# Gated DeltaNet decay matrices spread by TensorE, systems stored pair by pair, two solve steps per grain

## Chip, cores and metric

The kernel runs on one core of one Trainium2 chip. The metric is the device time of one execution in microseconds (us). Everything is float32; matmuls that are written with the type float32r take rounded operands, and a value is then carried as a rounded part and a remainder ("hi" and "lo").

## Reference, cut to what matters

A decoder trunk of two layers over 512 positions and 1024 features: windowed attention, feed-forward, gated DeltaNet, feed-forward. The change lies in the DeltaNet, which works on 16 heads (8 pairs that share a key head) and chunks of 64 positions:

```python
gc = jnp.cumsum(g, axis=-1)
decay = jnp.exp(jnp.where(incl, gc[..., :, None] - gc[..., None, :], -jnp.inf))
kk = jnp.einsum("bhncd,bhnsd->bhncs", k, k)
m = jnp.where(strict, beta[..., :, None] * kk * decay, 0.0)
a = m + jnp.eye(C, dtype=f32)
sol = lax.linalg.triangular_solve(a, rhs, left_side=True, lower=True, unit_diagonal=True)
qk = jnp.where(incl, jnp.einsum("bhncd,bhnsd->bhncs", q, k) * decay, 0.0)
# then a scan over the chunks: v_new = u - w S; o = q_dec S + qk v_new; S = S * g_last + k_dec^T v_new
```

## The kernel before, in words

Activations stand transposed, 128 features on the partitions and 512 positions along a row. Positions are cut into NB = 4 blocks of 128 (two chunks each).

**Dense work.** A weight tile of 128x1024 is loaded (L133), rounded by ScalarE (`whi`, L134), and VectorE makes the remainder (`wlo`, L135); `mm3` (L143) then issues three matmuls of 512 columns for each of 8 slices (L145, L146, L147), 24 to a tile. The three weight buffers turn over. The DeltaNet projects 48 such tiles in `gdn` (L653): 8 for k, then 24 for z and q in the order `zzqzzqzzqzzqzzzzzzzzqqqq` (L724), then 16 for v (L735). The output projection is 16 tiles in two halves (L741 to L768).

**Order.** Smaller jobs are Python generators in a queue. `dense` (L149) calls `pump` (L93) after every second slice, so a tile has four *grains*; a generator that yields n comes back n grains later. `until` (L102) pumps without dense work until something is ready. So the program order of the small jobs against the dense tiles is counted in grains; the tile framework turns program order, with its own estimate of what is ready, into one instruction order for each engine, which the chip then keeps. All loads and stores are issued by one queue, SP (SyncE).

**The jobs around the change.** `gates` (L576) makes the cumulated log decays `gc` (positions on partitions, blocks and heads along a row), turns them (L640) and stores the turned rows in DRAM as `rowd` (L644). `decays` (L772) then goes through the 8 pairs: four products of keys (`kk`, L807); for each of the two heads a DMA copies the head's 512 decays from `rowd` onto all 128 partitions of a buffer `D` (L799, one pair ahead; two buffers); VectorE subtracts `gc` and adds the mask `low` block by block (L810, 8 a pair); ScalarE takes the exponential of all 1024 columns at once (L812); `D` is stored (L813), multiplied into `kk` by VectorE (`kd`, L818) and stored (L820). A pair takes 6 grains (two times `yield 3`). `solve` (L825) loads the diagonal 32x32 blocks of all 16 heads and 8 chunks from the stored `kd` into `X` (L839, four DMAs, 128-byte pieces), scales them (L841), and makes 30 elimination steps of two VectorE instructions (L846, L848), one step a grain; then it stores the inverse and its transpose in a key-position layout (`T`, L854; `N`, L862). `recur` (L865) goes through the pairs: `prologue` (L888) loads `kk`, `D`, `kt`, `qd` (L900 to L903), waits for the solve and 16 grains more, loads `N` and `T` (L911, L914) and finishes the inverse with small matmuls (L923 to L961); it also waits for `rq`, which comes 10 grains after the last q tile, and for the pair's v; `chain` (L973) is the scan, `epilogue` (L1016) the gated norm. `post_qk` (L668) and `post_v` (L688) do convolution (L560 to L563), transposition (`turn`, L565) and norms for each projected tile.

Of the kernel before, what the change touches and what calls it, by code (L numbers as in the profile page):

```python
# [10 lines left out]
F32 = mybir.dt.float32  # L11
# [6 lines left out]
P = 128  # L18
T = 512
NB = 4  # L20
# [6 lines left out]
def layout(x, positions, mixer_norm, ffn_norm, attn_w_in, attn_q_gain, attn_k_gain, attn_sinks,  # L27
           attn_w_out, gdn_w_in, gdn_conv, gdn_a_log, gdn_dt_bias, gdn_norm, gdn_w_out,
           ffn_w_up, ffn_conv, ffn_conv_b, ffn_w_down):

    c = np.ascontiguousarray
    a = {}
    a["xT"] = c(x[0].T.reshape(KT, P, T))
    a["up"] = c(ffn_w_up.reshape(2, KT, P, 2, 24, P).transpose(0, 4, 3, 2, 1, 5)).reshape(2, 24, 2, P, 1024)
    a["down"] = c(ffn_w_down.reshape(2, 3, 8, P, 8, P).transpose(0, 1, 4, 3, 2, 5)).reshape(2, 3, 8, P, 1024)
    cols = []
    cols.append(mixer_norm.reshape(2, KT, P).transpose(2, 0, 1).reshape(P, 16))
    cols.append(ffn_norm.reshape(2, KT, P).transpose(2, 0, 1).reshape(P, 16))
    cols.append(ffn_conv.reshape(2, 3, 24, P).transpose(3, 0, 2, 1).reshape(P, 144))
    cols.append(gdn_conv[0].reshape(4, 32, P).transpose(2, 1, 0).reshape(P, 128))  # L40
    cols.append(gdn_norm[0].reshape(P, 1))
    cols.append(ffn_conv_b.reshape(2, 24, P).transpose(2, 0, 1).reshape(P, 48))
    w = attn_w_in[0]
    w = np.concatenate([w[:, 1024:1280], w[:, :512], w[:, 1280:], w[:, 512:1024]], axis=1)
    a["win"] = c(w.reshape(2, 4, P, 6, 256).transpose(3, 0, 2, 1, 4)).reshape(6, 2, P, 1024)
    wo = attn_w_out[0].reshape(2, 2, 4, 64, D).transpose(0, 2, 1, 3, 4).reshape(KT, P, KT, P)
    a["wout"] = c(wo.reshape(2, 4, P, KT, P).transpose(0, 3, 2, 1, 4)).reshape(2, KT, P, 512)
    a["rows"] = c(np.concatenate([attn_q_gain[0], attn_k_gain[0], attn_sinks[0]]))
    a["pos"] = c(positions[0].reshape(NB, P).T)
    a["freq"] = (500000.0 ** (-np.arange(0, 16, 2, dtype=np.float64) / 16)).astype(np.float32)  # L50
    i, j = np.arange(P)[:, None], np.arange(2 * P)[None]
    a["band"] = np.where((i + P - j >= 0) & (i + P - j < P), 0.0, -1e30).astype(np.float32)
    a["cols"] = c(np.concatenate(cols, axis=1))
    w = gdn_w_in[0].reshape(KT, P, -1).transpose(1, 0, 2)
    a["gin"] = c(w[:, :, :6144].reshape(P, KT, 48, P).transpose(2, 0, 1, 3)).reshape(48, P, 1024)
    a["gba"] = c(w[:, :, 6144:]).reshape(P, KT * 32)
    a["gout"] = c(gdn_w_out[0].reshape(2, 8, P, KT, P).transpose(0, 3, 2, 1, 4)).reshape(2, KT, P, 1024)
    a["grow"] = c(np.concatenate([gdn_a_log[0], gdn_dt_bias[0]]))
    a["tri"] = c(np.triu(np.ones((P, P), np.float32)))
    a["low"] = np.where(np.arange(P)[None] < np.arange(P)[:, None], -1e30, 0.0).astype(np.float32)  # L60
    a["ident"] = np.eye(P, dtype=np.float32)
    return a


# [3 lines left out]
class Builder:  # L68
# [507 lines left out]
    def gates(self, u, ready):  # L576
# [2 lines left out]
        V = nc.vector  # L579
        flat = lambda t: t.rearrange("p n h -> p (n h)")  # L580
        tri = gx.tile([P, P], F32, name="tri")
        self.low = gx.tile([P, P], F32, name="low")
        full = gx.tile([P, P], F32, name="full")
        grow = gx.tile([P, 32], F32, name="grow")
        self.aux.dma_start(tri, self.ins["tri"])
        self.aux.dma_start(self.low, self.ins["low"])
        self.aux.dma_start(grow, self.ins["grow"].partition_broadcast(P))
        V.memset(full, 1.0)
        hi, lo = self.weight(self.ins["gba"], 256)
        ps = self.psum()  # L590
        for k in range(KT):
# [48 lines left out]
        nc.tensor.transpose(pt[:, 0:P], both.rearrange("p i n h -> p (i n h)"), self.ident)  # L640
        bt = gx.tile([P, P], F32, name="bt")
        V.tensor_copy(bt, pt[:, 0:P])
        self.rowd = self.dram.tile([2, NB, 16, P], F32, name="rowd")
        self.aux.dma_start(self.rowd.rearrange("i n h c -> (i n h) c"), bt)  # L644
        ready.add("gates")
# [7 lines left out]
    def gdn(self, h, hd, stack, after):  # L653
# [5 lines left out]
        u, self.u = self.u, []  # L659
        d = self.d = {nm: dram(nm + "d", [8, P, 2, NB, P]) for nm in ("v", "z", "D")}  # L660
        d["kt"] = dram("ktd", [8, P, T])
        d["kk"], d["T"], d["N"] = dram("kkd", [P, 16, NB, P]), dram("Td", [P, 16, NB, 32]), dram("Nd", [P, 16, NB, 32])
        d["bk"] = dram("bkd", [2, 16, NB, 64])
        kT, qT = self.kT, self.qT = [], []
        ss = {"k": self.hub("ssk", 8), "q": self.hub("ssq", 8)}
# [43 lines left out]
        sp = st.enter_context(self.tc.tile_pool(name="sp", bufs=1, reuse_waits="tile"))  # L709
        sy = ExitStack()  # L710
        xp = sy.enter_context(self.tc.tile_pool(name="xp", bufs=1, side="right", reuse_waits="tile"))
        self.spawn(self.decays(sp, ready))
        self.spawn(self.solve(xp, ready))
        outs = {}

        def enter():
# [52 lines left out]
        st.close()  # L769
        return hp  # L770

    def decays(self, sp, ready):  # L772

        nc = self.nc
        V = nc.vector
# [17 lines left out]
        for m in range(2):  # L793
            self.aux.dma_start(d["bk"][m].rearrange("h n c -> n h c"), bt[:, m * 64:m * 64 + 64])

        def rows(hk):
            D = sp.tile([P, 2, NB, P], F32, tag="D", name="D", bufs=2)
            for j in range(2):
                self.aux.dma_start(D[:, j], self.rowd[0, :, 2 * hk + j].partition_broadcast(P))  # L799
            return D  # L800

        D = rows(0)
        for hk in range(8):
            kk = self.psum()
            for n in range(NB):
                s = slice(n * P, (n + 1) * P)
                nc.tensor.matmul(kk[:, s], self.kT[hk][:, s], self.kT[hk][:, s], start=True, stop=True)  # L807
            for j in range(2):
                for n in range(NB):
                    V.scalar_tensor_tensor(D[:, j, n], D[:, j, n], gc[:, n, 2 * hk + j:2 * hk + j + 1], self.low,  # L810
                                           op0=ALU.subtract, op1=ALU.add)
            nc.scalar.activation(D, D, AF.Exp)  # L812
            self.aux.dma_start(d["D"][hk], D)  # L813
            nxt = rows(hk + 1) if hk < 7 else None
            yield 3
            kd = sp.tile([P, 2, NB, P], F32, tag="kd", name="kd", bufs=2)
            for n in range(NB):
                V.scalar_tensor_tensor(kd[:, :, n], kk[:, n * P:(n + 1) * P].unsqueeze(1).broadcast_to([P, 2, P]), rk[:, n, hk:hk + 1],  # L818
                                       D[:, :, n], op0=ALU.mult, op1=ALU.mult)
            self.aux.dma_start(d["kk"][:, 2 * hk:2 * hk + 2], kd)  # L820
            D = nxt
            yield 3
        ready.add("systems")

    def solve(self, sp, ready):  # L825

        nc = self.nc
        V = nc.vector
        d = self.d
        while "systems" not in ready:  # L830
            yield 1
        X = sp.tile([P, 2, 32, 32], F32, name="X")
        bk = sp.tile([P, 2, 32], F32, name="bk")
        for m in range(2):
            ms = slice(m * 64, m * 64 + 64)
            self.aux.dma_start(bk[ms], d["bk"][m].rearrange("h n (i c) -> (h n) i c", i=2))
            for i in range(2):
                q = slice(m * 64 + i * 32, m * 64 + i * 32 + 32)
                self.aux.dma_start(X[ms, i], d["kk"][q, :, :, q].rearrange("s h n c -> (h n) s c"))  # L839
        for i in range(2):  # L840
            V.tensor_tensor(X[:, i], X[:, i], bk[:, i:i + 1].broadcast_to([P, 32, 32]), op=ALU.mult)  # L841
        yield 1
        for j in range(1, 31):
            w = 31 - j
            tm = sp.tile([P, 480], F32, name="tm")[:, :2 * j * w].rearrange("p (i s c) -> p i s c", i=2, c=w)
            V.tensor_tensor(tm, X[:, :, :j, j:j + 1].broadcast_to([P, 2, j, w]),  # L846
                            X[:, :, j:j + 1, j + 1:].broadcast_to([P, 2, j, w]), op=ALU.mult)
            V.tensor_tensor(X[:, :, :j, j + 1:], X[:, :, :j, j + 1:], tm, op=ALU.add)  # L848
            yield 1
        nc.gpsimd.memset(X.rearrange("p i s c -> p i (s c)")[:, :, ::33], 1.0)  # L850
        for m in range(2):
            for i in range(2):
                q = slice(m * 64 + i * 32, m * 64 + i * 32 + 32)
                self.aux.dma_start(d["T"][q].rearrange("s h n c -> (h n) s c"), X[m * 64:m * 64 + 64, i])  # L854
        for i in range(2):
            for b in range(2):
                nat = self.t2().rearrange("p (c s) -> p c s", s=32)
                cs = slice(b * 16, b * 16 + 16)
                nc.scalar.copy(nat, X[:, i, :, cs].rearrange("p s c -> p c s"))
                for m in range(2 - i):  # L860
                    q = slice(m * 64 + i * 32 + b * 16, m * 64 + i * 32 + b * 16 + 16)
                    self.aux.dma_start(d["N"][q].rearrange("s h n c -> (h n) s c"), nat[m * 64:m * 64 + 64])  # L862
        ready.add("solved")

    def recur(self, rx, ready, outs):  # L865
# [22 lines left out]
    def prologue(self, rx, hk, ready):  # L888
# [19 lines left out]
        for a in range(3):  # L908
            q = slice(a * 32, a * 32 + 32)
            c = slice(32, 64) if a == 1 else slice(0, 32)  # L910
            self.aux.dma_start(NT[q, :, :, c].rearrange("p j n c -> p (j n) c"), d["N"][q, hs].rearrange("p j n c -> p (j n) c"))  # L911
        for a in range(4):
            q = slice(a * 32, a * 32 + 32)
            self.aux.dma_start(TT[q, :, :, q].rearrange("p j n c -> p (j n) c"), d["T"][q, hs].rearrange("p j n c -> p (j n) c"))  # L914
        yield 3
        jn = [(j, n) for j in range(2) for n in range(NB)]

# [187 lines left out]
```

## Time and profile before

| | |
|---|---|
| time, median of 3 runs | 1582.84 us (1579.8 to 1583.84) |
| the profiled execution's own time | 1579.06 us |
| its span, first to last instruction | 1577.3 us |
| mean granted TensorE clock | 0.971 |
| DeltaNet, by its weight casts | about 577 to 1160 us of the span |

The page of the profile gives busy times of the engines, PE = TensorE's matmuls, PEld its weight loads, DVE = VectorE, ACT = ScalarE, POOL = GpSimd, SP = SyncE, and what ended each engine's idle time. "DVE D L810 <- DMA D<-rowd" reads: VectorE's instruction of line 810 that writes D waited for the DMA that writes D from rowd. Matmuls are pipelined, so the duration of one is longer than the distance from one to the next. A granted clock of 1.00 is 2.4 GHz; its lower level is 1.2 GHz, and a mean between shows how much of a stretch was at each.

### The profile page before, as it was taken

The numbers are of one execution on the slowest core, as the hardware profiler recorded it, in microseconds if no ns is written. First come the engines' busy times: TensorE is split into PE (matmuls) and PEld (weight loads), VectorE is DVE, ScalarE is ACT, GpSimd is POOL, SyncE is SP. The second block draws the span as 40 slices with busy tenths as digits, with TensorE's granted clock in tenths as the row PEclk, the third lists the DMA queues.
The fourth block names the chain that finished last, engine by engine and source line by source line (L and its number), as shares of the span: only waits on it lengthen the run. The fifth ranks groups of instructions, "written<-read, shape, count | busy, mean of one in ns | idle before, by whom it ended". The sixth has DMA issues, their size and how long they took to land. (4 is left out here: it accounts for less than half of the span.)

```text
span 1577.3 us, 20933 instructions
## 1 busy us (share of the span) xinstructions
PE 1494.1 (95%) x7914; PEld 1229.2 (78%) x7914; DVE 903.7 (57%) x1818; ACT 677.8 (43%) x1515; POOL 10.4 (1%) x21
## 2 busy tenths in 40 slices
PE   7989999999999999977788999989999999999998
PEld 7965788888888888756566888777788888888887
DVE  7586766446545558653478555555466545644652
ACT  7686743233223336533335456543443323322331
POOL 0000000000000000000000000000000000000000
PEclk9999999999999999988999999989999999999999
DMA  5111322322233243464675646545132232233232
GB/s 187 57 28 34 101 93 94 106 95 94 94 99 102 96 145 110 118 192 166 176 225 118 209 145 170 149 130 130 54 95 92 95 106 94 93 100 101 95 100 74
DMA packets 104572, 179.96 MB, mean 114 GB/s; under 512 B 45336, under 2 KB 57624, under 8 KB 104472
## 3 DMA queue, kind: packets, MB, share of 16 engines
q1 hardware_dynamic: 104472, 178.63, 37.7%
q8 instruction: 62, 1.02, 0.3%
q14 instruction: 38, 0.31, 0.1%
HBM read 153.60 MB, written 25.00 MB: 113 GB/s over the span
## 5 line engine op out<-in xcount | busy, mean ns | idle before, releaser
L147 PE MATMUL ps<-a,wlo 128*128 128x512 f32 x1736 | 685.3, 395 | 28.3 <-DVE wlo L135 28.2
L145 PE MATMUL ps<-a,whi 128*128 128x512 f32 x1736 | 695.1, 401 | 8.0 <-ACT whi L134 6.8
L146 PE MATMUL ps<-a,whi 128*128 128x512 f32 x1736 | 683.8, 394 | 0.0
L134 ACT CAST whi<-raw 128x1024 fp32r<-128x1024 f32 (+1 forms) x239 | 242.6, 1016 | 464.4 <-PE ps L146 394.9
L147 PEld LDWEIGHTS ps<-a,wlo 128*128 128x128 f32 x1736 | 329.4, 190 | 102.2 <-DVE wlo L135 32.0
L145 PEld LDWEIGHTS ps<-a,whi 128*128 128x128 f32 x1736 | 329.9, 190 | 81.5 <-ACT whi L134 7.6
L146 PEld LDWEIGHTS ps<-a,whi 128*128 128x128 f32 x1736 | 330.0, 190 | 66.6 <-DVE a L141 0.8
L135 DVE TENSOR_TENSOR wlo<-raw,whi 128x1024 fp32r<-128x1024 f32 (+1 forms) x239 | 280.4, 1174 | 60.9 <-ACT whi L134 57.4
L255 DVE TENSOR_TENSOR h<-h,ps 128x512 f32<-128x512 f32 x48 | 33.0, 688 | 148.5 <-PE ps L147 148.5
L240 DVE TENSOR_TENSOR t<-ps,rbc 128x512 f32<-128x512 f32 x48 | 33.2, 691 | 106.6 <-PE ps L147 106.4
L246 DVE TENSOR_TENSOR t<-ps,rbc 128x512 f32<-128x512 f32 x48 | 33.2, 692 | 90.8 <-PE ps L147 90.8
L244 ACT ACTIVATE t<-t 128x512 f32<-128x512 f32 x48 | 30.4, 632 | 98.0 <-DVE t L243 98.0
L145 PE MATMUL ps<-whi,a 128*128 128x256 f32 x192 | 56.7, 296 | 8.5 <-ACT a L189 8.5
L146 PE MATMUL ps<-wlo,a 128*128 128x256 f32 x192 | 55.1, 287 | 0.5 <-DVE wlo L135 0.5
L147 PE MATMUL ps<-whi,a 128*128 128x256 f32 x192 | 55.0, 287 | 0.0
L810 DVE SCALAR_TENSOR_TENSOR D<-D,both,low 128x128 f32<-128x128 f32 x64 | 18.1, 347 | 60.3 <-DMA D<-rowd 56.3
L145 PEld LDWEIGHTS ps<-whi,a 128*128 128x128 f32 x192 | 37.4, 195 | 10.5 <-ACT a L189 8.5
L562 DVE SCALAR_TENSOR_TENSOR t<-ps,cols,t 128x511 f32<-128x511 f32 (+2 forms) x48 | 35.6, 746 | 17.4 <-ACT t L560 13.7
L140 ACT CAST a<-t 128x512 fp32r<-128x512 f32 x48 | 30.0, 625 | 32.9 <-DVE t L247 32.9
L241 ACT ACTIVATE t<-t,cols 128x512 f32<-128x512 f32 x48 | 38.9, 811 | 2.0 <-DVE t L240 2.0
L146 PEld LDWEIGHTS ps<-wlo,a 128*128 128x128 f32 x192 | 37.6, 196 | 0.7 <-DVE wlo L135 0.7
L147 PEld LDWEIGHTS ps<-whi,a 128*128 128x128 f32 x192 | 37.4, 195 | 0.1
(245 smaller groups left out, 1417.6 us busy)
## 6 DMA issues: line engine op xcount, KB each, us to landing
raw<-in_up SPq DMA_DIRECT2D x96, 512.0 KB, 3.7
raw<-in_down SPq DMA_DIRECT2D x48, 512.0 KB, 3.6
raw<-in_gin SPq DMA_DIRECT2D x48, 512.0 KB, 4.4
raw<-in_gout SPq DMA_DIRECT2D x16, 512.0 KB, 4.4
raw<-in_win SPq DMA_DIRECT2D x10, 512.0 KB, 4.3
raw<-in_wout SPq DMA_DIRECT2D x16, 256.0 KB, 2.7
zd<-t SPq DMA_DIRECT2D x16, 256.0 KB, 4.8
D<-rowd SPq DMA_DIRECT2D x16, 256.0 KB, 11.9
```

Of the source, the lines that this page charges most:

```text
L134: nc.scalar.copy(hi[:, s], raw[:, s])
L135: nc.vector.tensor_tensor(lo[:, s], raw[:, s], hi[:, s].bitcast(F32), op=ALU.subtract)
L140: nc.scalar.copy(hi, src)
L145: mm(ps, w[0], x[0], start=first, stop=False)
L146: mm(ps, w[0], x[1], start=False, stop=False)
L147: mm(ps, w[1], x[0], start=False, stop=last)
L240: nc.vector.tensor_tensor(g, gu[0], self.bc, op=ALU.mult)
L241: nc.scalar.activation(y, g, AF.Identity, bias=self.col(C_FB + l * 24 + j), scale=self.col(cw + 2))
L244: nc.scalar.activation(y, y, AF.Silu)
L246: nc.vector.tensor_tensor(t, gu[1], self.bc, op=ALU.mult)
L255: nc.vector.tensor_tensor(h[m], h[m], ps, op=ALU.add)
L562: nc.vector.scalar_tensor_tensor(dst[:, i:], g[:, :T - i], self.col(cw + 3 - i), dst[:, i:], op0=ALU.mult, op1=ALU.add)
```

## The change

Decay rows no longer go through DRAM for `decays`. `gates` also keeps `bt` times a column mask per block as two rounded operands `rows2` (hi and lo) of 128x512, made by ScalarE and VectorE; a selector matrix `sel` from the host gives, for each head, the column that picks that head's rows. For each head three matmuls of 512 columns sum into one PSUM bank: identity times the mask `low`, and the head's selector, repeated over 128 columns, times each part of `rows2`. ScalarE reads that bank in four instructions and takes the exponential with `-gc` (`ngc`) as its per-partition bias. The pair's diagonal blocks are stored into `X`'s layout as soon as `kd` exists, four DMAs a pair; `X`, `T` and `N` have the layout of the solve in DRAM, and the prologue's loads pick their pieces out of it. A pair takes 4 grains and the solve two steps a grain.

```diff
+    r = np.arange(P)
+    sel = [(r // 16 == n) for n in range(NB)] + [(r < 64) & (r % 16 == h) for h in range(16)]
+    a["sel"] = c(np.stack(sel, axis=1).astype(np.float32))
...
+        self.lowr, self.identr = gx.tile([P, P], F32R, name="lowr"), gx.tile([P, P], F32R, name="identr")
+        self.selr = gx.tile([P, 16], F32R, name="selr")
+        nc.scalar.copy(self.lowr, low)
+        nc.scalar.copy(self.identr, self.ident)
+        nc.scalar.copy(self.selr, sel[:, 4:])
...
+        self.rows2 = [self.a2().rearrange("p (n c) -> p n c", n=NB) for _ in range(2)]
+        hi, lo = self.rows2
+        for n in range(NB):
+            nc.scalar.activation(hi[:, n], bt, AF.Copy, scale=sel[:, n:n + 1])
+            V.scalar_tensor_tensor(lo[:, n], bt, sel[:, n:n + 1], hi[:, n].bitcast(F32), op0=ALU.mult, op1=ALU.subtract)
+        self.ngc = self.hub("ngc")
+        V.tensor_scalar(self.ngc, self.gc, -1.0, None, op0=ALU.mult)
...
-        d["kk"], d["T"], d["N"] = dram("kkd", [P, 16, NB, P]), dram("Td", [P, 16, NB, 32]), dram("Nd", [P, 16, NB, 32])
+        d["kk"] = dram("kkd", [P, 16, NB, P])
+        d["X"], d["T"], d["N"] = (dram(nm, [2, 64, 2, 32, 32]) for nm in ("Xd", "Td", "Nd"))
...
-        def rows(hk):
-            D = sp.tile([P, 2, NB, P], F32, tag="D", name="D", bufs=2)
-            for j in range(2):
-                self.aux.dma_start(D[:, j], self.rowd[0, :, 2 * hk + j].partition_broadcast(P))
-            return D
-
-        D = rows(0)
+        low4 = self.lowr.unsqueeze(1).broadcast_to([P, NB, P])
         for hk in range(8):
             kk = self.psum()
...
+            D = sp.tile([P, 2, NB, P], F32, tag="D", name="D", bufs=2)
             for j in range(2):
+                h = 2 * hk + j
+                pd = self.psum()
+                one = self.selr[:, h:h + 1].to_broadcast([P, P])
+                nc.tensor.matmul(pd, self.identr, low4, start=True, stop=False)
+                nc.tensor.matmul(pd, one, self.rows2[0], start=False, stop=False)
+                nc.tensor.matmul(pd, one, self.rows2[1], start=False, stop=True)
                 for n in range(NB):
-                    V.scalar_tensor_tensor(D[:, j, n], D[:, j, n], gc[:, n, 2 * hk + j:2 * hk + j + 1], self.low,
-                                           op0=ALU.subtract, op1=ALU.add)
-            nc.scalar.activation(D, D, AF.Exp)
+                    nc.scalar.activation(D[:, j, n], pd[:, n * P:(n + 1) * P], AF.Exp, bias=self.ngc[:, n, h:h + 1])
             self.aux.dma_start(d["D"][hk], D)
-            nxt = rows(hk + 1) if hk < 7 else None
-            yield 3
+            yield 2
...
+            for m in range(2):
+                for i in range(2):
+                    q = slice(m * 64 + i * 32, m * 64 + i * 32 + 32)
+                    self.aux.dma_start(d["X"][m, 8 * hk:8 * hk + 8, i].rearrange("(j n) s c -> s j n c", j=2), kd[q, :, :, q])
             self.aux.dma_start(d["kk"][:, 2 * hk:2 * hk + 2], kd)
-            D = nxt
-            yield 3
+            yield 2
...
-            for i in range(2):
-                q = slice(m * 64 + i * 32, m * 64 + i * 32 + 32)
-                self.aux.dma_start(X[ms, i], d["kk"][q, :, :, q].rearrange("s h n c -> (h n) s c"))
+        self.aux.dma_start(X, d["X"].rearrange("m p i s c -> (m p) i s c"))
...
             V.tensor_tensor(X[:, :, :j, j + 1:], X[:, :, :j, j + 1:], tm, op=ALU.add)
-            yield 1
+            if j % 2 == 0:
+                yield 1
...
-        for m in range(2):
-            for i in range(2):
-                q = slice(m * 64 + i * 32, m * 64 + i * 32 + 32)
-                self.aux.dma_start(d["T"][q].rearrange("s h n c -> (h n) s c"), X[m * 64:m * 64 + 64, i])
+        self.aux.dma_start(d["T"].rearrange("m p i s c -> (m p) i s c"), X)
...
-                for m in range(2 - i):
-                    q = slice(m * 64 + i * 32 + b * 16, m * 64 + i * 32 + b * 16 + 16)
-                    self.aux.dma_start(d["N"][q].rearrange("s h n c -> (h n) s c"), nat[m * 64:m * 64 + 64])
+                self.aux.dma_start(d["N"].rearrange("m p i c s -> (m p) i c s")[:, i, cs], nat)
...
-            self.aux.dma_start(NT[q, :, :, c].rearrange("p j n c -> p (j n) c"), d["N"][q, hs].rearrange("p j n c -> p (j n) c"))
+            self.aux.dma_start(NT[q, :, :, c].rearrange("p j n c -> p (j n) c"),
+                               d["N"][a // 2, 8 * hk:8 * hk + 8, a % 2].rearrange("p c s -> c p s"))
...
-            self.aux.dma_start(TT[q, :, :, q].rearrange("p j n c -> p (j n) c"), d["T"][q, hs].rearrange("p j n c -> p (j n) c"))
+            self.aux.dma_start(TT[q, :, :, q].rearrange("p j n c -> p (j n) c"),
+                               d["T"][a // 2, 8 * hk:8 * hk + 8, a % 2].rearrange("p s c -> s p c"))
```

## Rows read from the trace of the kernel before

**Rows 1.** The page: busy time of each engine, and the granted clock in 40 slices.

```profile
PE 1494.1 (95%) x7914; PEld 1229.2 (78%) x7914; DVE 903.7 (57%) x1818; ACT 677.8 (43%) x1515; POOL 10.4 (1%) x21
PEclk9999999999999999988999999989999999999999
```

**Rows 2.** Stretches: length, busy (x instructions) of PE, PEld, DVE, ACT, POOL; clock, DMA.

```profile
520.00:580.00 60.00, 60.00 (x267) 49.67 (x266) 34.75 (x44) 23.64 (x31) 0.00 (x0) 1.00 0.38 123
680.00:780.00 100.00, 69.15 (x278) 54.42 (x278) 44.43 (x100) 35.87 (x69) 2.14 (x3) 0.83 0.56 182
780.00:860.00 80.00, 69.04 (x299) 55.84 (x297) 56.69 (x93) 33.07 (x71) 0.22 (x1) 0.95 0.70 178
985.00:1157.00 172.00, 155.50 (x1178) 131.21 (x1177) 96.40 (x245) 82.92 (x252) 3.78 (x6) 0.93 0.42 115
```

**Rows 3.** Waits in 680 to 780 us: waiter, what ended it, us in total, times, longest.

```profile
DVE D L810 <- DMA D<-rowd: 46.3, 9, 11.9
PE ps L147 <- DVE wlo L135: 28.2, 6, 10.9
PE ps L145 <- ACT whi L134: 1.7, 1, 1.7
```

**Rows 4.** VectorE in order of time, 685 to 704 us: start, us, instruction.

```profile
696.94 1.14 DVE L810 SCALAR_TENSOR_TENSOR D<-D,both,low 128x128 f32<-128x128 f32 x4 [11.87 <-DMA D<-rowd]
...
702.63 1.22 DVE L135 TENSOR_TENSOR wlo<-raw,whi 128x1024 fp32r<-128x1024 f32 x1
```

**Rows 5.** TensorE in order of time, 688 to 705 us.

```profile
688.72 1.05 PE L807 MATMUL ps<-a 128*128 128x128 f32 x8
...
703.90 0.80 PE L147 MATMUL ps<-a,wlo 128*128 128x512 f32 x1 [10.94 <-DVE wlo L135]
```

**Rows 6.** Windows 680 to 780 us of lines L147, L807 and L570 alone, one row each.

```profile
680.00:780.00 100.00, 33.86 (x74) 16.15 (x74) 0.83 0.56 182
...
680.00:780.00 100.00, 6.61 (x43) 6.65 (x42) 0.83 0.56 182
...
680.00:780.00 100.00, 1.85 (x12) 1.42 (x12) 0.83 0.56 182
```

**Rows 7.** ScalarE reading 128x128 of a PSUM bank (L696), and the present exponential (L812).

```profile
L696 ACT ACTIVATE t<-ps,beta x64: 352/368/401, 861.6 to 1037.8; 128x128 f32<-128x128 f32 x64
...
L812 ACT ACTIVATE D<-D x8: 1056/1057/1062, 675.4 to 775.0; 128x1024 f32<-128x1024 f32 x8
```

**Rows 8.** SP's issues, min/median/max ns: T pieces, kd, z and raw.

```profile
L914 SPq DMA_DIRECT2D TT<-Td x32: 303/446/1632, 864.7 to 1089.8; - x32
...
L820 SPq DMA_DIRECT2D kkd<-kd x8: 319/1492/3840, 682.4 to 777.8; - x8
...
L733 SPq DMA_DIRECT2D zd<-t x16: 319/400/3767, 650.9 to 815.5; - x16
...
L133 SPq DMA_DIRECT2D raw<-in_gin x48: 327/333/4200, 563.3 to 939.9; - x48
```

**Rows 9.** DMA issues by line: KB each, median us to landing.

```profile
zd<-t SPq DMA_DIRECT2D x16, 256.0 KB, 4.8
...
Td<-X SPq DMA_DIRECT2D x4, 256.0 KB, 5.0
```

**Rows 10.** VectorE by line, 785 to 860 us (the solve): busy us, mean ns.

```profile
L848 DVE TENSOR_TENSOR X<-X,tm 128x60 f32<-128x60 f32 (+14 forms) x30 | 15.0, 500 | 0.6
L846 DVE TENSOR_TENSOR tm<-X 128x60 f32<-128x60 f32 (+14 forms) x30 | 15.0, 500 | 0.7
L135 DVE TENSOR_TENSOR wlo<-raw,whi 128x1024 fp32r<-128x1024 f32 x10 | 12.2, 1220 | 5.2 <-ACT whi L134 5.0
```

**Rows 11.** TensorE's waits in 780 to 870 us, and its longest in 985 to 1160 us.

```profile
PE ps L570 <- ACT t L563: 6.3, 1, 6.3
PE ps L145 <- ACT whi L134: 5.0, 1, 5.0
...
PE ps L934 <- DVE x L927: 10.0, 4, 3.9
```

More of the change, by code (lines that the diff above doesn't have):

```diff
@@ L581, in gates @@
         tri = gx.tile([P, P], F32, name="tri")
-        self.low = gx.tile([P, P], F32, name="low")
+        low = gx.tile([P, P], F32, name="low")
+        sel = gx.tile([P, 20], F32, name="sel")
         full = gx.tile([P, P], F32, name="full")
@@ L585, in gates @@
         self.aux.dma_start(tri, self.ins["tri"])
-        self.aux.dma_start(self.low, self.ins["low"])
+        self.aux.dma_start(low, self.ins["low"])
+        self.aux.dma_start(sel, self.ins["sel"])
         self.aux.dma_start(grow, self.ins["grow"].partition_broadcast(P))
         V.memset(full, 1.0)
+        self.lowr, self.identr = gx.tile([P, P], F32R, name="lowr"), gx.tile([P, P], F32R, name="identr")
[3 more added lines that the diff above has]
+        nc.scalar.copy(self.selr, sel[:, 4:])
         hi, lo = self.weight(self.ins["gba"], 256)
@@ L711, in gdn @@
         xp = sy.enter_context(self.tc.tile_pool(name="xp", bufs=1, side="right", reuse_waits="tile"))
-        self.spawn(self.decays(sp, ready))
-        self.spawn(self.solve(xp, ready))
+        X = xp.tile([P, 2, 32, 32], F32, name="X")
+        self.spawn(self.decays(sp, X, ready))
+        self.spawn(self.solve(xp, X, ready))
         outs = {}
@@ L770, in gdn, with decays @@
         return hp
-    def decays(self, sp, ready):
+    def decays(self, sp, X, ready):
         nc = self.nc
@@ L819, in decays, with solve @@
                                        D[:, :, n], op0=ALU.mult, op1=ALU.mult)
+            for m in range(2):
+                for i in range(2):
+                    q = slice(m * 64 + i * 32, m * 64 + i * 32 + 32)
+                    self.aux.dma_start(d["X"][m, 8 * hk:8 * hk + 8, i].rearrange("(j n) s c -> s j n c", j=2), kd[q, :, :, q])
             self.aux.dma_start(d["kk"][:, 2 * hk:2 * hk + 2], kd)
-            D = nxt
-            yield 3
+            yield 2
         ready.add("systems")
-    def solve(self, sp, ready):
+    def solve(self, sp, X, ready):
         nc = self.nc
@@ L831, in solve @@
             yield 1
-        X = sp.tile([P, 2, 32, 32], F32, name="X")
         bk = sp.tile([P, 2, 32], F32, name="bk")
```

## The prediction

> **What bounds the kernel now.** The page comes first: TensorE is busy 95% of the span, no other engine over 57%, and the granted clock dips only in a few slices in the middle, in the DeltaNet [rows 1]. So what counts is what stops TensorE or adds work to it. Next the stretches. In the feed-forward 60 us hold 267 matmuls at full clock: 60/267 = 0.225 us each, 5.4 us for a tile of 24. In 680 to 780 us, where the decays are made, TensorE is busy for 69 of 100 us and the mean clock is 0.83 [rows 2]. The waits of that stretch name the cause: TensorE waits for `wlo` 28.2 us and for `whi` 1.7 us, and VectorE itself waits 46.3 us for the broadcast decay rows [rows 3]. Two timelines show the link. VectorE stands 11.87 us before a subtraction of line 810, and `wlo`, which is behind it, starts at 702.63 [rows 4]; TensorE stands 10.94 us for that `wlo` and runs again at 703.90, its matmul twice as long as usual [rows 5]. The granted clock has then fallen to its lower level, 1.2 GHz: a mean of 0.83 is (1 - 0.83)/0.5 = 34 of 100 us at that level.
>
> How much is lost there I take from the work done. The stretch holds 74 matmuls of line 147, so 3 x 74 = 222 of 512 columns, 49.9 us at 0.225; 43 records of line 807, eight of which take 1.05 us, 5.6 us [rows 5, 6]; 12 transpositions, 1.9 us [rows 6]. That is 57.4 us of work in 100, so about 42 us are lost: 30 us of waits and some 12 us of running at the lower clock.
>
> **The change part by part.**
>
> *Decay rows on TensorE.* The 64 subtractions and the waits before them go, and with them the cause of the 42 us. TensorE gets 8 pairs x 2 heads x 3 = 48 matmuls of 512 float32r columns, the kind of line 147: 48 x 0.225 = 10.8 us, all on the engine that sets the end. Their weight loads lie beside matmuls as those of the dense tiles do (PEld 49.67 of 60 us while PE is always busy [rows 2]). Net -31 us.
>
> *Exponentials.* ScalarE gets 64 reads of 128x128 from PSUM at most 0.37 us each, 23.6 us, for 8 x 1.06 = 8.5 us that go [rows 7]: +15 us, costed at nothing, because ScalarE is busy 36 of 100 us there [rows 2]. A pair now lasts 4 grains, 5.4 + 1.05 + 6 x 0.225 = 7.8 us; its ScalarE work (a cast of 1 us, 8 x 0.37, and in one tile of three a convolution's share) stays under that. If the cover is gone, `whi` is late and TensorE waits for it. The two banks more per pair are released by these reads; the set-up in `gates` (twelve short instructions, one more load) happens once beside dense tiles. Costed at nothing.
>
> *Stores by pair.* SP issues per pair raw, z, `kd` and now four small stores of 256 pieces of 128 bytes, the size of the loads of line 914, while two broadcasts go: 0.33 + 0.40 + 1.49 + 4 x 0.45 = 4.0 us, and some 0.3 us for D, of 7.8 [rows 8]. Behind them waits the next raw tile; it has the three weight buffers as cover. Bounds: nothing, and 18 us a pair if each issue costs the row's maximum (a rival below). I take nothing, since half of all issues cost the median or less. For the landing, 256 KB in pieces of 128 bytes take 5.0 us to land and 256 KB of z in long ones 4.8 [rows 9]. The Trainium skill, "DMA: Bandwidth & Descriptors", Specifications, speaks against this part: below 512 bytes a transfer is a read-modify-write and misses line rate. By that rule, taken as twice the landing (an estimate), a pair's stores and N's loads would come 5 us later each, ten in all on the path to line 923, and the sum below would be -26; the trace's two landings do not bear it out.
>
> *Earlier solve.* Counted in grains: gates are ready at 41, the first pair stands at 44. Before, 8 x 6 grains lead to 92 ("systems"), 31 more to 123 (solved), and the chain of the first pair starts at 152. After, 8 x 4 lead to 76, 16 more to 92; the prologue then stops at `rq`, whose q tile ends at 128 and which comes at 139, and the chain starts at 146. Of 31 grains 6 are kept. A pair's chain has 11 grains and its epilogue 7; v's tiles end at 192. `until` then pumps without dense work 5 + 7 + 5 = 17 grains before, 0 + 6 + 5 = 11 after. In 985 to 1157 us TensorE is idle 16.5 us, and 24 us are at the lower clock, which costs at most 12 [rows 2]; its longest wait there is for small VectorE steps [rows 11]. Six of 17 is 6 to 10 us; none of it if those gaps come from the chain itself. I take -5.
>
> *What is late next.* The two solve instructions a step are 30.0 us of VectorE [rows 10], now in 15 grains, 20 us of dense work. And the small matmuls that need N (line 923) stand 36 grains after "systems", 9 tiles or 49 us. Their data need: last pair's store 5 us, X's load (1 MB) some 6, the solve 30 + 2.4 of scaling, nine `wlo` between its steps at 1.22 [rows 10], 11 us, then copies, store and load some 11: 65 us. If TensorE's order keeps the program's place, it waits 16 us there and some 3 more at the lower clock; if the order puts them later, nothing. The row nearest is that of before, where the same path cost no wait of its own [rows 11]. I take +8, nearer to the middle, because the margin of 50 grains that it had there shrinks to 36. Against it stand two waits around the old solve, 5.0 us for a late `raw` behind X's four scattered loads and 6.3 us behind a pile of ScalarE work at the solve's end [rows 11], some 5 us more at the lower clock (80 x 0.05/0.5 = 8 us [rows 2]): 0 to 16 us. The scattered loads go, so I take -8.
>
> **Sum.** -42 + 10.8 - 5 + 8 - 8 = -36 us against the profiled execution's 1579.06: 1543. That execution lies 3.8 us under the median 1582.84, on whose scale I predict **1547 us**. Differences under 0.3% (4.7 us) can't be told from no change.
>
> **Rivals.**
>
> *Better: the old waits around the solve go entirely and N is in time.* -31 - 10 - 16 = -57: 1526 to 1535. For it: the pile of ScalarE work falls among z tiles. Against it: the solve has half the dense work to hide in. Chance 0.17.
>
> *The solve becomes the wait.* TensorE stands at line 923 for the full 19 us, or `wlo` queues behind the solve's steps (32.4 + 4 x 1.22 - 21.6 = 16 us). With one of them and nothing else won, -31 + 19 = -12: 1571; with both, no change. For it: VectorE is busy 57 of 80 us there already [rows 2]. Against it: TensorE's two waits while the old solve ran were not for `wlo` [rows 11]. Chance 0.12, a third of it within 0.3%.
>
> *SP's queue, the slower side.* If the pair's stores are issued at the maxima of rows 8, raw 4.2 + z 3.8 + `kd` 3.8 + 4 x 1.63 = 18 us against 7.8 of work, the next raw comes late in each pair: 8 x 10.5 = 84 us, 1631. It turns the forecast to slower from 7.8 + 36/8 = 12.3 us a pair. Against it: the median issues sum to 4.0. Chance 0.05. (The new matmuls at line 807's rate, 1.05 us for 512 columns, would make 50 us instead of 10.8, and 1587: 0.01 more.)
>
> *The change does not do what it says:* the 28 us come from crowded DMA in general, and `wlo` stays late through raw tiles. Then only half returns: -21 + 11 = -10 to 0. Against it: rows 3 name rowd for 46 us. Chance 0.04.
>
> **How the numbers follow.** The forecast has 0.61 (its own range 1537 to 1559). Faster: 0.61 + 0.17 + 0.08 + 0.01 = 0.87; same: 0.04 + 0.03 = 0.07; slower 0.06. The range reaches into the better case and the solve's wait: 1529 to 1569.
>
> **What would show it.** Right: no wait of VectorE for rowd in the decays; eight pairs in about 65 us from 660, granted clock 1.00 there; 48 new matmuls at 0.225 us from one to the next; "systems" near 726 instead of 778 us. The solve's last step 60 us later, and line 923's wait between 0 and 19 us. Wrong: `wlo` or `whi` still named by TensorE's waits in the decays, SP's issues over 8 us a pair, new matmuls at 1 us, or a lower clock in 660 to 730.

## The result, and the profile after

The changed kernel takes 1552.14 us (median; 1546.77 to 1555.39) where the kernel before, on the same chip, takes 1581.32: a ratio of 0.982, 95% interval 0.980 to 0.984, so 29.2 us less. The profiled execution is at 1552.91, 26.2 under that of before. First the page of the changed kernel, its busy row and the granted clock in 40 slices (in rows 1 before).

```profile
PE 1488.9 (96%) x7962; PEld 1228.9 (79%) x7962; DVE 890.0 (57%) x1759; ACT 686.7 (44%) x1576; POOL 10.4 (1%) x21
...
PEclk9998999999999999999979998999999999999999
```

The two slices at 0.8 in the decays (18 and 19, about 670 to 749 us [rows 1]) are gone, and a new dip stands in slice 21 (about 775 to 814 us). Now stretches of the changed kernel, in the columns of rows 2: the decays, the dip, and the whole recurrence.

```profile
660.00:730.00 70.00, 69.47 (x342) 58.11 (x341) 34.00 (x73) 45.44 (x116) 2.15 (x3) 1.00 0.64 214
783.40:800.50 17.10, 5.47 (x41) 4.08 (x42) 3.53 (x9) 7.81 (x11) 0.00 (x0) 0.50 0.84 274
805.00:1130.00 325.00, 302.15 (x2260) 255.00 (x2259) 188.96 (x428) 166.70 (x492) 7.88 (x13) 0.96 0.42 129
```

The decays are now one block without a gap: 69.47 busy of 70 us, at full clock. In the dip the clock is at its lower level, 1.2 GHz, and TensorE is busy 5.5 of 17.1 us. What it waits for most between 600 and 860 us:

```profile
PE ps L938 <- DMA NT<-Nd: 14.4, 1, 14.4
PE ps L1010 <- DMA vb<-vd: 2.5, 1, 2.5
PE ps L148 <- ACT whi L137: 2.3, 1, 2.3
```

`wlo` is gone from the list [rows 3], and so is the pile of ScalarE work [rows 11]. A new wait leads: line 938 (line 923 before) needs N. The timeline of TensorE in the changed kernel shows a pair's new matmuls and this wait:

```profile
665.80 0.40 PE L827 MATMUL ps<-a,selr 128*128 128x512 f32 x1
666.03 0.40 PE L828 MATMUL ps<-a,selr 128*128 128x512 f32 x1
666.27 0.40 PE L826 MATMUL ps<-lowr,identr 128*128 128x512 f32 x1
...
780.22 0.39 PE L150 MATMUL ps<-a,wlo 128*128 128x512 f32 x1
795.03 0.31 PE L938 MATMUL ps<-NT,kk 32*32 32x32 f32 x2 [14.43 <-DMA NT<-Nd]
795.27 0.80 PE L148 MATMUL ps<-a,whi 128*128 128x512 f32 x1
```

A decay matmul starts 0.23 to 0.24 us after the one before it. At 780.22 the dense work ahead of line 938 is used up, and the dense matmul behind the wait takes twice its time. VectorE's timeline and SP's (`SPq` issues) tell why N comes only at 795:

```profile
784.77 0.26 DVE L865 TENSOR_TENSOR X<-X,tm 128x60 f32<-128x60 f32 x1
```
```profile
786.40 2.27 SPq L875 DMA_DIRECT2D Nd<-t  x3
788.81 3.30 SPq L752 DMA_DIRECT2D zd<-t  x5
792.16 1.90 SPq L924 DMA_DIRECT2D NT<-Nd  x3
```

The solve's last step starts at 784.77, 4.2 us after TensorE stopped (780.60), and 10.3 us of stores and loads follow it. Last, the landings (KB each, median us from issue) between 660 and 730 us, before the change and after:

```profile
raw<-in_gin SPq DMA_DIRECT2D x7, 512.0 KB, 14.5
D<-rowd SPq DMA_DIRECT2D x12, 256.0 KB, 11.9
Dd<-D SPq DMA_DIRECT2D x5, 512.0 KB, 6.2
```
```profile
Dd<-D SPq DMA_DIRECT2D x8, 512.0 KB, 2.7
...
raw<-in_gin SPq DMA_DIRECT2D x7, 512.0 KB, 4.3
...
Xd<-kd SPq DMA_DIRECT2D x32, 32.0 KB, 1.7
```

Without the broadcasts of `rowd` the weights (`raw`) land in 4.3 us instead of 14.5, and D's store in 2.7 instead of 6.2. The prediction looked at those who wait for rows, not at their neighbours in the DMA engines; this is what the experiments had to separate.

### The profile page after: what moved, and what is told of

Read it like the earlier page. It is cut to its first block, busy times and chain, and to the rows that moved or that the text cites. A ratio compares the mean times of both kernels' runs of the same rounds, so it can differ in the third digit from the quotient of the medians.

```text
span 1551.0 us, 21045 instructions
## 1 busy us (share of the span) xinstructions
PE 1488.9 (96%) x7962; PEld 1228.9 (79%) x7962; DVE 890.0 (57%) x1759; ACT 686.7 (44%) x1576; POOL 10.4 (1%) x21
## 4 chain that ended last, share of the span: by engine, by line
PE 85%; DVE 5%; DMA 5%; ACT 4%; issue 1%; SPq 0%; POOL 0%; DVEq 0%
PE ps L148 25%; PE ps L149 25%; PE ps L150 25%; DMA qd<-rowd 3%; ACT sc L520 1%; PE ps L573 1%; DVE wlo L138 1%; PE ps L545 1%; PE ps L961 1%; PE ps L1010 1%; DVE sc L514 1%; PE ps L1017 1%; PE ps L1003 1%; PE ps L1019 1%; PE ps L511 1%
## 5 line engine op out<-in xcount | busy, mean ns | idle before, releaser
L148 PEld LDWEIGHTS ps<-whi,a 128*128 128x128 f32 x192 | 38.0, 198 | 11.2 <-ACT a L192 9.1
L246 DVE SCALAR_TENSOR_TENSOR t<-t,cols,t 128x510 f32<-128x510 f32 x48 | 36.0, 750 | 1.7
```

What stands on the lines that cost most here:

```text
L148: mm(ps, w[0], x[0], start=first, stop=False)
L246: nc.vector.scalar_tensor_tensor(y[:, 2:], g[:, :T - 2], self.col(cw), y[:, 2:], op0=ALU.mult, op1=ALU.add)
```

## The experiments

Times are medians; each ratio is to the kernel before, on the same chip.

**The new wait.** Two ways to take it away: the readers of N 12 grains later, or the solve 15 grains longer.

```
-            yield 16
+            yield 28
```

> The changed kernel, with the prologue's pause after the solve 28 grains long and no longer 16, so that the small matmuls that read N stand 12 grains (16 us of dense work) later in TensorE's order; the scan waits for rq anyway. Theory (the 14.4 us wait for N is a new wait of its own, paid at the end): the wait goes and with it the stretch at the lower clock behind it, some 3 us, so 17 us less than the changed kernel, about 1535 us. Rival (the wait only shows a lateness that the recurrence would meet anywhere): the same 14 us turn up as a wait at the first scan or as pumping without dense work, 1550 to 1552 us.

Measured: 1532.28 us, ratio 0.9715 (0.9685 to 0.9744). TensorE's waits, 660 to 860 us, e1:

```profile
PE ps L938 <- DMA NT<-Nd: 1.1, 1, 1.1
```

```
-            if j % 2 == 0:
-                yield 1
+            yield 1
```

> The changed kernel with one solve step a grain, as before, all else changed. Theory (two steps a grain buy nothing, since the steps run as fast as VectorE can and the scan waits for rq; they only move the readers of N 15 grains nearer): the wait for N goes, the solve's last step comes within 5 us of where it was, about 1535 us. Rival (the denser steps are what brings the solve forward): the solve ends some 20 us later and the time is at 1552 us or above.

Measured: 1531.80 us, ratio 0.9705 (0.967 to 0.974). Lines 863 and 865 are the solve; the group of line 865 (ns min/median/max, first and last start), in the changed kernel and in e2:

```profile
L865 DVE TENSOR_TENSOR X<-X,tm x30: 223/540/658, 739.3 to 784.8; 128x60 f32<-128x60 f32 x2, 128x116 f32<-128x116 f32 x2, 128x168 f32<-128x168 f32 x2, 128x216 f32<-128x216 f32 x2
```
```profile
L865 DVE TENSOR_TENSOR X<-X,tm x30: 223/539/657, 738.5 to 784.7; 128x60 f32<-128x60 f32 x2, 128x116 f32<-128x116 f32 x2, 128x168 f32<-128x168 f32 x2, 128x216 f32<-128x216 f32 x2
```

With one step a grain the solve ends at the same time: the grains don't set its pace. Two steps a grain only bring N's readers 15 grains nearer. By the ratios this costs 0.011, 17 us, and the changed kernel is better without it.

**The parts alone.** e3 is the kernel before with rows by TensorE and nothing else (old stores, 6 grains a pair, one step a grain); e4 is the kernel before with X, T and N in the solve's layout and the broadcasts kept; e10 is e3 with the systems earlier, 4 grains a pair.

```
-            nc.scalar.activation(D, D, AF.Exp)
+                nc.tensor.matmul(pd, self.identr, low4, start=True, stop=False)
+                nc.tensor.matmul(pd, one, self.rows2[0], start=False, stop=False)
+                nc.tensor.matmul(pd, one, self.rows2[1], start=False, stop=True)
...
+                    nc.scalar.activation(D[:, j, n], pd[:, n * P:(n + 1) * P], AF.Exp, bias=self.ngc[:, n, h:h + 1])
```

> The kernel before with the decay rows on TensorE alone: 6 grains a pair, one solve step a grain, X, T and N by the old DMAs. Theory (the loss in the decays was VectorE standing for the broadcast rows): 42 us go and 10.8 come, 1550 us, with the two old waits around the solve (5.0 and 6.3 us) still in it. Rival (crowded DMA in general kept the weight tiles late): at most half returns, 1570 us, and TensorE still names wlo in the decays.

Measured: 1539.24 us, ratio 0.9766 (0.9733 to 0.98): the rows alone gain 37 us, more than the whole change and 6 more than the theory's 31. The two old waits were to stay, but only one is left. TensorE's only wait in e3 between 670 and 880 us:

```profile
PE ps L573 <- ACT t L566: 8.1, 1, 8.1
```

The 5.0 us wait for `whi` [rows 11] is gone although e3 still has X's four scattered loads, so it went with the rows on TensorE and not with those loads.

```
+                    self.aux.dma_start(d["X"][m, 8 * hk:8 * hk + 8, i].rearrange("(j n) s c -> s j n c", j=2), kd[q, :, :, q])
...
-                self.aux.dma_start(X[ms, i], d["kk"][q, :, :, q].rearrange("s h n c -> (h n) s c"))
+        self.aux.dma_start(X, d["X"].rearrange("m p i s c -> (m p) i s c"))
```

> The kernel before with X, T and N in the layout of the solve and X stored pair by pair, the broadcast rows kept. Theory (the layout only relieves the load of X and the stores after the solve): VectorE's waits for the rows stay near 46 us, TensorE's 5.0 us wait behind X's loads goes, 1574 to 1580 us. Rival (small stores in the middle of the decays crowd the queue that the rows share): the rows land later still and the time rises, 1585 to 1600 us.

Measured: 1584.02 us, ratio 1.005 (1.0034 to 1.0065): slower, as the rival had it, though less than its range. Its cause is not borne out: between 660 and 800 us the rows landed in 10.9 us here and in 11.9 before, and VectorE's wait for them is 60.0 us for 56.3 (660 to 860 us). What comes late are the weights. TensorE's waits of e4 in 660 to 860 us, and SP's issues of raw tiles:

```profile
PE ps L145 <- ACT whi L134: 39.0, 4, 24.2
PE ps L147 <- DVE wlo L135: 7.8, 2, 7.3
```
```profile
681.87 0.35 SPq L133 DMA_DIRECT2D raw<-in_gin  x1
...
734.22 0.33 SPq L133 DMA_DIRECT2D raw<-in_gin  x1
```

No weights are asked for in 52 us: between these two lines SP issues the stores and broadcasts of the pairs and a few z tiles, and they stand ahead of the next raw tile.

```
-            yield 3
+            yield 2
```

(for e10, twice in the loop over the pairs of e3)

> Decay rows on TensorE, 4 grains a pair, one solve step a grain, but X, T and N by the old DMAs. Theory (what the version with one step has over the decay rows alone, 7 us, comes from the earlier start, which moves the pile of ScalarE work at the solve's end in among z tiles): 1530 to 1534 us. Rival (it comes from the new layout of X, T and N): 1538 to 1542 us.

Measured: 1542.75 us, ratio 0.9772 (0.9746 to 0.9798), the same as e3. TensorE's first wait between 720 and 880 us:

```profile
PE ps L940 <- DMA NT<-Nd: 9.9, 1, 9.9
```

Systems that are ready 16 grains sooner gain nothing with the old stores: the 8.1 us behind the pile of ScalarE work go, and N comes late instead. e10 and e2 differ in the layout alone, so in an otherwise changed kernel the layout is worth 0.0067 by the ratios, 11 us (the intervals allow 4 to 17), which is about this wait; on the kernel before it costs 0.005. So the change is made of -37 for the rows, nothing for the earlier systems, -11 for the layout and +17 for two steps a grain: -31, for 29 measured.

**What the broadcasts cost.** e5 is e2 with the 16 broadcasts put back into a buffer that nothing reads; e8 the same, issued by GpSimd, so that SP's order is that of e2.

```
+            G = sp.tile([P, 2, NB, P], F32, tag="G", name="G", bufs=2)
+            for j in range(2):
+                self.aux.dma_start(G[:, j], self.rowd[0, :, 2 * hk + j].partition_broadcast(P))
```

> The version with one solve step a grain (1531.8 us), with the 16 broadcasts of the decay rows put back into a buffer that nobody reads; the output is unchanged. Theory (the loss came from engines standing in order behind the rows, not from their traffic): 1532 to 1537 us, no wait for wlo or whi over 3 us in the decays. Rival (broadcasts and small stores crowd the queue, as the layout alone did on the old kernel): raw tiles late, TensorE waiting 15 to 40 us for whi, 1547 to 1575 us.

Measured: 1578.07 us, ratio 1.002 (1.0001 to 1.0041): 46 us over e2, more than the rival's range, lost to rows that no engine waits for. Waits of e5 in 660 to 800 us, and SP's issues:

```profile
PE ps L148 <- ACT whi L137: 40.2, 3, 34.2
ACT whi L137 <- DMA raw<-in_gin: 38.2, 6, 27.9
```
```profile
656.91 0.63 SPq L136 DMA_DIRECT2D raw<-in_gin  x1
...
721.83 2.04 SPq L136 DMA_DIRECT2D raw<-in_gin  x1
```

```
-                self.aux.dma_start(G[:, j], self.rowd[0, :, 2 * hk + j].partition_broadcast(P))
+                nc.gpsimd.dma_start(G[:, j], self.rowd[0, :, 2 * hk + j].partition_broadcast(P))
```

> The unread broadcasts again, on the version with one solve step a grain, but issued by GpSimd's queue, so that the order of SP's own loads and stores is the one without them. Theory (what the broadcasts cost is the place that they and the raw tiles get in SP's one queue): 1532 to 1537 us, raw tiles issued every 8 us or so. Rival (their bytes crowd the 16 DMA engines and raw tiles land late wherever they are issued): 1550 to 1578 us as before.

Measured: 1557.60 us, ratio 0.9862 (0.9829 to 0.9895), inside the rival's range: of the 46 us about 20 come back with SP's order and 26 stay (25 and 25 by the ratios). Landings of e8, 660 to 730 us:

```profile
G<-rowd POOLq DMA_DIRECT2D x16, 256.0 KB, 12.9
Dd<-D SPq DMA_DIRECT2D x5, 512.0 KB, 15.8
raw<-in_gin SPq DMA_DIRECT2D x4, 512.0 KB, 12.3
```

So the transfers beside the broadcasts are slow, D's store 15.8 us instead of 2.7. It reaches the engines through buffers: VectorE stands for `kd`, whose stores have not landed (e8, 660 to 860 us):

```profile
DVE kd L838 <- DMA Xd<-kd: 20.4, 2, 12.3
```

That the 26 us are the traffic alone is not shown, for the queue is another too. The row of the same stretch of e8, and that of e2:

```profile
660.00:730.00 70.00, 54.94 (x260) 44.39 (x259) 22.45 (x47) 28.46 (x71) 12.01 (x16) 0.93 0.88 175
```
```profile
660.00:730.00 70.00, 69.47 (x343) 58.09 (x342) 34.02 (x71) 44.64 (x112) 2.15 (x3) 1.00 0.63 215
```

The DMA engines are busier (0.88 against 0.63) and move less (175 against 215 GB/s).

e11 was to tell whether it is the repetition of one row: the same unread loads from 128 different rows of a weight.

```
-                nc.gpsimd.dma_start(G[:, j], self.rowd[0, :, 2 * hk + j].partition_broadcast(P))
+                nc.gpsimd.dma_start(G[:, j], self.ins["down"][1, 2, hk][:, 512 * j:512 * j + 512].rearrange("p (n c) -> p n c", n=NB))
```

> As the unread broadcasts on GpSimd's queue (1557.6 us against 1531.8 without them), but each 256 KB comes from 128 different rows of a weight in DRAM and no longer from one row that all partitions repeat; the output is unchanged. Theory (a broadcast is dear because every partition reads the same 2 KB): 1532 to 1540 us, the tiles of D landing in 3 to 5 us. Rival (it is the bytes, and the queue that they are issued from): 1553 to 1560 us, D landing in over 10 us.

Measured: 1533.69 us, ratio 0.9724 (0.9699 to 0.9749), as the theory wanted; but the run doesn't test it. A weight is there from the start, so these loads had nothing to wait for. Their issues (ns min/median/max, first and last start):

```profile
L834 POOL DMA_DIRECT2D G<-in_down x16: 536/536/670, 110.2 to 126.5; - x16
```

And over the whole kernel the packets, MB and share of 16 engines' span of GpSimd's queue, with the landing of its loads, in e11 and in e8:

```profile
q0 software_dynamic: 1280, 4.20, 0.8%
...
G<-in_down POOLq DMA_DIRECT2D x16, 256.0 KB, 3.5
```
```profile
q0 software_dynamic: 1280, 4.20, 2.4%
```

They went at 110 to 126 us, far from the decays. What the run gives is a price: as many packets and bytes took 0.8% of 1531.9 us, 12 us of all 16 engines, where the repeated rows took 2.4% of 1556.9, 37 us. The stretch differs, and so does the form (2 KB of a row in one piece against four of 512 bytes), so repetition is the likely cause and is not shown.

**Broadcasts kept, but earlier or elsewhere.** e7 is the kernel before with rows asked for three pairs ahead, in four buffers; e9 the kernel before with its broadcasts issued by GpSimd.

```
+        ahead = [rows(i) for i in range(3)]
...
+            D = ahead.pop(0)
...
-            nxt = rows(hk + 1) if hk < 7 else None
+            if hk < 5:
+                ahead.append(rows(hk + 3))
```

> The kernel before with the rows' broadcasts issued three pairs ahead into four buffers, nothing else changed, so no matmuls are added. Theory (the rows were only issued too late): VectorE's 46 us of waits go to under 10, 42 us less, near 1539 us. Rival (the broadcasts land as slowly as they do because of their own traffic and of what stands in the queue with them): the rows or the raw tiles stay late, 1560 to 1580 us.

Measured: 1567.37 us, ratio 0.9954 (0.9936 to 0.9972), as the rival had it. VectorE still waits for rows, about half as long; in 660 to 860 us of the kernel before and of e7:

```profile
DVE D L810 <- DMA D<-rowd: 56.3, 13, 11.9
```
```profile
DVE D L811 <- DMA D<-rowd: 30.6, 9, 8.2
```

```
-                self.aux.dma_start(D[:, j], self.rowd[0, :, 2 * hk + j].partition_broadcast(P))
+                nc.gpsimd.dma_start(D[:, j], self.rowd[0, :, 2 * hk + j].partition_broadcast(P))
```

> The kernel before with its decay rows still broadcast from DRAM and read by VectorE, issued by GpSimd's queue; no matmuls added. Theory (SP's queue): VectorE's waits for the rows fall from 56 us to under 20, TensorE's waits in the decays to under 10, 1540 to 1552 us. Rival (traffic): the rows land in 12 us as before and the time stays at 1570 us or above.

Measured: 1601.34 us, ratio 1.014 (1.0107 to 1.0173). The rival holds: the rows land in 12.8 us between 660 and 800 us. VectorE's waits for them and TensorE's waits in e9, 660 to 860 us:

```profile
DVE D L810 <- DMA D<-rowd: 45.1, 10, 9.4
DVE D L810 <- issue: 36.6, 4, 11.8
```

```profile
PE ps L147 <- DVE wlo L135: 27.9, 5, 9.8
PE ps L145 <- ACT whi L134: 23.0, 3, 8.6
```

VectorE stands 81.7 us before line 810, where it stood 60.3 before, 56.3 of it for the rows; "issue" means that the profile shows nothing it waited for, so what holds it in those 36.6 us is open. `wlo` is as late as before [rows 3], and the wait for `whi`, 6.8 us in the same stretch of the kernel before, is 23.0. Why this is worse than the kernel before is otherwise open.

**The price of the matmuls.** e6 is e2 with the mask added four times a head, 48 matmuls more; the exponential of a masked place is 0 either way.

```
-                nc.tensor.matmul(pd, self.identr, low4, start=True, stop=False)
+                for r in range(4):
+                    nc.tensor.matmul(pd, self.identr, low4, start=r == 0, stop=False)
```

> The same version with the mask's matmul issued four times for each head, 48 more matmuls of 512 columns; the mask's sum is four times as far below zero and the output is unchanged. Theory (TensorE sets the end in the decays): 48 x 0.225 = 10.8 us more, 1542.6 us. Rival (they fill idle time): 1532 to 1535 us; rival (they go at the rate of the key products, 1.05 us each): 1582 us.

Measured: 1542.64 us, ratio 0.9792 (0.9755 to 0.9829). The medians of e6 and e2 lie 10.8 us apart, as 48 x 0.225 wants; by the ratios it is 14, and the intervals allow some us either way.

**A better version.** e2's recurrence still broadcasts: `qd` of each pair of heads comes from `rowd`. VectorE's wait for it in 780 to 1100 us of e2:

```profile
DVE qd L971 <- DMA qd<-rowd: 26.3, 6, 6.6
```

e12 makes `qd` as the decays are made:

```
-        self.aux.dma_start(qd, self.rowd[1, 1:, hs].partition_broadcast(P))
+        for j in range(2):
...
+            one = self.selr[:, h:h + 1].to_broadcast([P, P])
+            nc.tensor.matmul(pe[:, :3 * P], one, self.rows2[0][:, 1:], start=True, stop=False)
+            nc.tensor.matmul(pe[:, :3 * P], one, self.rows2[1][:, 1:], start=False, stop=True)
+            nc.scalar.activation(qd[:, :, j], pe[:, :3 * P].rearrange("p (n c) -> p n c", c=P), AF.Exp)
```

> The version with one solve step a grain, with the prologue's broadcast of exp(gc) (384 KB a pair from rowd) also made by TensorE, two matmuls of 384 columns a head, and ScalarE's exponential. Theory (the broadcasts cost wherever they are: VectorE stood 18.5 us for this one between 820 and 1000 us): 32 matmuls of 0.17 us, 5.4 us, come and more than that goes, 1522 to 1529 us. Rival (off the path there): 5 us more, 1535 to 1540 us.

Measured: 1511.67 us, ratio 0.9586 (0.9558 to 0.9615), the fastest of all, and more than expected. The profiled execution of e2 is its longest (1539.19 us, median 1531.8), so e11 stands beside it, which has the same recurrence and was profiled at 1533.65. The stretch 860 to 985 us in e2, e11 and e12, and the granted clock of e12:

```profile
860.00:985.00 125.00, 114.02 (x914) 97.30 (x913) 71.64 (x164) 68.89 (x209) 4.75 (x7) 0.92 0.49 144
```
```profile
860.00:985.00 125.00, 113.82 (x968) 96.62 (x969) 75.34 (x181) 72.76 (x221) 4.75 (x7) 0.96 0.53 154
```
```profile
860.00:985.00 125.00, 122.81 (x1077) 105.18 (x1076) 83.50 (x197) 91.97 (x252) 5.04 (x8) 1.00 0.48 151
```
```profile
PEclk9998999999999999999999999999999999999999
```

TensorE is idle 2.2 us there instead of 11, and the clock, 0.92 and 0.96 without the change, stays at 1.00. Which part of the 20 us is VectorE's wait and which the other transfers was not separated.

## Why the prediction was right, and where it was not

The time lies 5 us over the forecast and inside its range; it is faster, as the forecast's cases had it. The sum came to -28 for -36 (below): the wait for N missed by 9 us, the two small terms by 2 and 3 in opposite ways. That these two nearly cancel is luck.

- *The loss in the decays, -42: held in size.* No wait for rows, `wlo` in time, the clock at 1.00, eight pairs in about 63 us where 65 were forecast. *Its cause held only in part.* The prediction named VectorE standing in order, and gave 0.04 to crowding in general. e5 loses 46 us although no engine waits for its rows: some 20 us with the place that raw tiles get in SP's order (e8 against e5), 26 us with the same loads from another queue (e8 against e2). This is measured in the changed kernel; how the 42 us of the kernel before divide between VectorE's order and the broadcasts' cost to others is not shown. e7 asks for rows three pairs ahead instead of one and still has 30.6 us of VectorE's wait. The size could hold with a cause held in part because the change takes the broadcasts away, and with them every cost that they had.
- *Matmuls, +10.8: held*, in the starts of the timeline (48 x 0.234 = 11.2) and in e6.
- *The wait for N, +8: the step that failed.* It took 14.4 us and, with 5.5 us of work at the lower clock, some 2.7 more: 17. The prediction's own path gave 65 us of data need against 49 of work, so 16 and 3; from the last pair's store, about 726, to 795 it is 69. It then halved that because the same path cost nothing before [rows 11]. That row could not bear it out: before, 50 grains stood between. e1 and e2 take the wait away and gain 17 us by their ratios, so what the rival priced as "the solve becomes the wait" came true almost in full.
- *The old waits around the solve, -8: more came, and not for the reason given.* In 780 to 860 us before, TensorE was idle 11.0 us and ran 5.5 us at the lower clock (summed over stretches of 1 us), which loses 2.7: 13.7 in all. 2.3 are left, so some 11 were gained. The prediction gave them to the scattered loads of X. e3 and e10 keep these and have no wait for `whi`; the 5.0 us went with the broadcast rows, and the 6.3 us with the earlier systems, since the pile of ScalarE work still costs 8.1 us in e3 and nothing in e10.
- *Fewer empty grains, -5: not as idle time, some 3 by the clock.* Over the whole recurrence TensorE was idle 21.2 us before and 22.9 after, by the row of before below and the 805 to 1130 us row above; the prediction named this case, gaps that come from the chain itself. But the mean clock rose from 0.94 to 0.96: TensorE ran 34.7 us at the lower clock before and 25.0 after (summed over stretches of 1 us), and half of the difference is gained, which with the idle time makes some 3 us.

The row of before, in the same columns:

```profile
860.00:1157.00 297.00, 275.83 (x2182) 232.55 (x2183) 171.95 (x410) 151.61 (x448) 7.87 (x13) 0.94 0.50 139
```

The measured terms make -42 + 10.8 + 17 - 11 - 3 = -28, for 26.2 between the profiled executions and 29.2 between the medians.

- *Stores by pair, nothing: held.* The four stores of a pair landed in 1.7 us each, SP issued them at a median of 0.45 us, and N's loads, issued from 792.16, were there by 795.03. The Trainium skill, "DMA: Bandwidth & Descriptors", Specifications, states that a transfer below 512 bytes is a read-modify-write and misses line rate. The prediction's estimate by it, twice the landing, made -26; the time is near that, but by the path to N as a whole: the landings that can be compared, 5.0 us in short pieces against 4.8 in long ones [rows 9], show no doubling.

## What to carry to other kernels

Price a broadcast of a DRAM row over the partitions by what it does to its neighbours in the DMA engines and in its queue, not only by who waits for it; an unread copy of the transfer measures that. A row spread by TensorE cost it here three matmuls of 512 columns a head, 0.23 us each, and ScalarE's reads of PSUM found room. Before giving a producer fewer grains, look at what sets its pace: if the grains don't, only its reader moves nearer; and keep the full data path as the forecast for that reader, rather than a margin that the change has used up. And check in an experiment's trace when its added work ran, before reading its time.

## What was not expected of the hardware

256 KB read from one decay row to 128 partitions took 12.9 us to land (e8), against 3.5 for 256 KB from 128 different rows in another stretch (e11), and with the former under way 512 KB of D took 15.8 us to store instead of 2.7. A busy share of the DMA engines is therefore no measure of bytes: 0.88 of them moved 175 GB/s in e8, 0.63 of them 215 in e2.
